# Sample attention: a batch's own tokens weighted through a zeroed 128-wide tile instead of a 16-row slice

## The chip, the cores and the metric

The kernel runs on one core of one Trainium2 chip. The metric is the device time of one execution in microseconds (us). The kernel before took 1886.86 us (median of three runs, 1886.31 to 1892.37).

The names used below: PE is TensorE, DVE is VectorE, ACT is ScalarE, POOL is GpSimd, and SP is the engine that issues nearly all transfers.

## The reference

One step of a two-layer streaming encoder (half-step FFN, a token mixer with four branches, half-step FFN) for 256 prompt frames and for 8 sample streams ("batches") of 16 frames each. The change lies in one branch of the mixer, the latent attention of the sample streams:

```python
def mla_sample(q_nope, q_rope, lat_all, kr_all, w_ukv):
    k_nope, v = mla_expand(lat_all, w_ukv)
    prob = jax.nn.softmax(mla_scores(q_nope, q_rope, k_nope, kr_all), axis=-1).astype(v.dtype)
    return jnp.einsum('bhqk,bkhd->bqhd', prob, v).reshape(b, t, W_A)
# lat_all = concatenate([cache_lat (256 past latents), latent (16 own latents)], axis=1), per batch
```

Each of the 8 batches therefore has 8 heads x 16 frames = 128 query rows, and each row weights 256 cached latents and the 16 latents of its own batch, 256 numbers wide. The products with the key and value matrices are absorbed before and after, so that what is computed per batch is softmax(scores) times latents.

## The kernel before, in words

All 384 frames (256 prompt, 128 sample) go through the layer together. Large products run on PE as three passes of a split in two fp32r halves (`mm3`, line 304): in the trace they are the matmuls `rot<-xh,wh`, `rot<-xh,wl`, `rot<-xl,wh`, 128x384. Every weight block is loaded to a staging buffer by SP (`st`, line 224), cast on ACT (`wh<-st`) and subtracted on DVE (`wl<-st,wh`).

The sample attention is in plain fp32, and one such matmul shows in the trace as two records. The stage lies in `mixer_front`, after the attention of the prompt, and comes once in each layer (from 396 to 460 us and from 1328 to 1392 us). For each batch b (two groups `c` of four):

- `load_ct` (lines 1099 to 1104) loads the cached latents `ct` (256 x 256), and copies the batch's 16 rows of `lat_s` (128 rows: 8 batches x 16) by a transfer into a tile `nl` that begins at partition 0.
- The scores of 128 rows x 272 columns (`acc<-cT,qa`, then `acc<-ck,qrs`) go to one PSUM bank. POOL copies the own latents into the last 16 columns of `cT` before.
- `sample` (line 1109) takes the softmax: row maximum on DVE, exp on ACT, reciprocal and scaling on DVE, into a `half` tile.
- `sample_out` (line 1117) turns the weights: three PE transposes (`acc<-ident,half`, the last one of 16 columns), a copy of 128x256 on ACT and one of 16x128 on DVE to `pTs`; then, for each of two halves of the latent, two matmuls with `ct` over 128 rows and one with `nl` over 16 rows, all three adding up in one PSUM tile; ACT copies the result to `qa`.

The order of work is written out by the program itself: every step is a generator that yields the engine it waits for, and a queue of due times (`tick`, `step`, `ready`, with the costs of `COST` and `LATENCY`) decides at which point of PE's stream it goes on. Between the steps, `fillers` (projections and the first gates, as `rot` passes) run on PE, and the 62 taps of a depthwise convolution (`yTb<-bs,cols,yTb`) fill DVE. The engines PE, ACT, DVE and POOL run in just this order; SP takes its transfers in the order in which they become ready by the planner, and a transfer also waits until the one eight before it has landed, since eight semaphores go round.

Of the kernel before, what the change touches and what calls it, by code (L numbers as in the profile page):

```python
# [8 lines left out]
F32 = mybir.dt.float32  # L9
F32R = mybir.dt.float32r  # L10
BF16 = mybir.dt.bfloat16
AF = mybir.ActivationFunctionType
ALU = mybir.AluOpType
AX = mybir.AxisListType
PSUM = bass.MemoryType.PSUM

P = 128
# [9 lines left out]
S = 16  # L27
NP = TP // S
PAST = 256
# [4 lines left out]
KL = 256  # L34
# [12 lines left out]
PE, ACT, DVE, POOL = "tensor", "scalar", "vector", "gpsimd"  # L47
# [50 lines left out]
class Core:  # L98
# [537 lines left out]
    def mixer_front(self, l, m, mf, ma, aT, yT):  # L636
        nc, tc, a = self.nc, self.tc, self.a
        mm = nc.tensor.matmul
# [10 lines left out]
        lat_s = ma.tile([P, KL], F32, name="lat_s")  # L649
# [187 lines left out]
        with pool("mixq") as mq:  # L837
# [122 lines left out]
            for hp in range(4):  # L960
                w = self.weights(("uq", l, hp))
                for i in range(2):
                    h = 2 * hp + i
                    o = self.bank()[:, :T]
# [22 lines left out]
            for j in range(4):  # L987
                o = self.bank()[:, :TP]
# [5 lines left out]
            for t in range(2):  # L994
                o = self.bank()
# [49 lines left out]
            def load_cT(b, pool=None):  # L1045
                if pool:
                    cTs[b] = pool.tile([P, 2, PAST + S], F32, tag="cT", name="cT", bufs=3)
                else:
                    x = self.gains.tile([P, D], F32, tag="g", name="cT")
                    cTs[b] = x[:, :2 * (PAST + S)].rearrange("p (k s) -> p k s", k=2)  # L1050
                nc.sync.dma_start(out=cTs[b][:, :, 0:PAST], in_=a["cacheT"][l, b])
# [8 lines left out]
            for i in range(4):  # L1060
# [3 lines left out]
                                  in_=krT[64:96, TP:].rearrange("p (c i s) -> p c i s", c=2, i=4)[:, :, i, :])  # L1064
# [9 lines left out]
        with pool("mixs") as ms:  # L1074

            def absorb(k, g, o):
                yield PE
                for i in range(2):
                    dst = qa[:, k].rearrange("p b (h i s) -> p h i b s", h=4, i=2)[:, 2 * g:2 * g + 2, i]
                    src = o[i][:, :2 * P].rearrange("p (h b s) -> p h b s", h=2, b=NB)  # L1080
                    for j in range(2):
                        (nc.vector.tensor_copy if j else nc.scalar.copy)(dst[:, j], src[:, j])

            qa = ms.tile([P, 2, NB, H * S], F32, name="qa")
            for k in range(2):
                for g in range(2):
                    o = [self.bank() for _ in range(2)]
                    for j in range(2):
                        for i in range(2):
                            mm(o[i][:, j * P:(j + 1) * P], lhsT=wkT[i * 64:(i + 1) * 64, 2 * g + j, k * P:(k + 1) * P],  # L1090
                               rhs=qTs[i * 64:(i + 1) * 64, 2 * g + j, :], start=True, stop=True)
                    self.spawn(("qa",), absorb(k, g, o), "acc")
            wuv = ma.tile([P, 2, 512], F32, tag="w", name="wuv")
            nc.sync.dma_start(out=wuv, in_=a["w_ukv"][l, 1])
            self.wait(("qa",), fillers)

            cts = {}

            def load_ct(b):
                ct = ms.tile([P, 2, KL], F32, tag="ct", name="ct", bufs=4)  # L1100
                nc.sync.dma_start(out=ct, in_=a["cache"][l, b].rearrange("(k p) c -> p k c", p=P))
                nl = ms.tile([S, KL], F32, tag="nl", name="nl", bufs=4)
                nc.sync.dma_start(out=nl, in_=lat_s[b * S:(b + 1) * S, :])
                cts[b] = ct, nl

            for b in range(2, 5):
                load_cT(b, ms)

            def sample(b, sb):
                ct, nl = cts.pop(b)  # L1110
                yield PE
                p = self.half()[:, :PAST + S].unsqueeze(1)
                yield from self.softmax(p, sb.unsqueeze(1), 1)
                self.drop("acc")
                self.spawn(("att",), sample_out(b, p, ct, nl))

            def sample_out(b, p, ct, nl):
                yield DVE
                pt = self.acc(2, 0)
                for k in range(2):  # L1120
                    nc.tensor.transpose(pt[:, k * P:(k + 1) * P], p[:, 0, k * P:(k + 1) * P], self.ident)
                nc.tensor.transpose(pt[0:S, 256:384], p[:, 0, PAST:], self.ident)
                self.drop("half")
                yield PE
                ps = ms.tile([P, 3, P], F32, tag="pTs", name="pTs", bufs=2)
                nc.scalar.copy(ps[:, 0:2, :], pt[:, 0:256].rearrange("p (a b) -> p a b", a=2))
                nc.vector.tensor_copy(ps[0:S, 2, :], pt[0:S, 256:384])
                self.drop("acc")
                yield ACT
                o = self.acc(2, 1)[:, :256].rearrange("p (a b) -> p a b", a=2)  # L1130
                for k in range(2):
                    ksl = slice(k * P, (k + 1) * P)
                    for kc in range(2):
                        mm(o[:, k, :], lhsT=ct[:, kc, ksl], rhs=ps[:, kc, :], start=(kc == 0), stop=False)
                    mm(o[:, k, :], lhsT=nl[:, ksl], rhs=ps[0:S, 2, :], start=False, stop=True)
                yield PE
                nc.scalar.copy(qa[:, :, b, :], o)

            for c in range(2):
                sbs = []  # L1140
                for i in range(4):
                    b = 4 * c + i
                    cT = cTs.pop(b)
                    load_ct(b)
                    nc.gpsimd.tensor_copy(cT[:, :, PAST:], latTs[:, :, b * S:(b + 1) * S])
                    sb = self.acc(i // 2, i % 2)[:, :PAST + S]
                    sbs.append(sb)
                    for k in range(2):
                        mm(sb, lhsT=qa[:, k, b, :], rhs=cT[:, k, :], start=(k == 0), stop=False)
                    if 2 <= b < NB - 3:  # L1150
                        load_cT(b + 3, ms)
                    if i == 1:
                        self.pull(fillers, PACE_S)
                for i in range(4):
                    rg = slice(32 * i, 32 * i + 32)
                    mm(sbs[i], lhsT=qrs[rg, c, :], rhs=ck[rg, c, :], start=False, stop=True)
                for i in range(4):
                    self.spawn(("soft",), sample(4 * c + i, sbs[i]), "acc")
                    self.pull(fillers, PACE_S)
                self.wait(("soft",), fillers)  # L1160
            self.wait(("att",), fillers)
            def attended(j, o):
                yield PE
                nc.vector.tensor_copy(aT[:, j, TP:], o)

            for j in range(4):
                o = self.bank()[:, :P]
                for i in range(2):
                    h = 2 * j + i
                    for k in range(2):  # L1170
                        mm(o[i * 64:(i + 1) * 64, :], lhsT=wuv[:, k, h * 64:(h + 1) * 64],
                           rhs=qa[:, k, :, h * S:(h + 1) * S], start=(k == 0), stop=(k == 1))
                self.spawn(("att",), attended(j, o), "acc")
# [311 lines left out]
```

## Time and profile before

| | |
|---|---|
| median of the runs | 1886.86 us |
| the profiled execution | 1885.2 us, its span 1883.4 us |
| PE busy | 1858.1 us (99% of the span) |
| DVE, ACT, POOL busy | 964.1, 693.3, 73.8 us |
| granted PE clock | 0.999 of full speed over the span |

The profile is of one execution. "Busy" of PE counts matmuls that overlap: a record lasts from its start to the end of its pipeline, so that the step from one record to the next, and not the record's length, tells what it costs in a stream. In the timeline, equal records that follow each other are merged into one row with their number.

### The profile page before, as it was taken

To read this page: it belongs to the slowest core of one execution; us is meant where nothing else is said; L and a number is where in the kernel's file an instruction comes from. 1 tells how busy PE (TensorE), PEld (TensorE's weight loads), DVE (VectorE), ACT (ScalarE), POOL (GpSimd) and SP (SyncE) were. 2 spreads that over 40 slices of the span, in tenths; PEclk is the share of its full clock that TensorE was granted. 3 is DMA by queue.
4 is the path that set the end of the run, shared out by engine and by line. 5 is a ranking of instruction groups with operands and counts; after the bars stand their busy time and mean duration, and the time that the engine had idled before them with its cause. 6 is when DMAs were issued, how large, how long until landed. Compare 5 with 4: busy or idle time off the path is not lost.

```text
span 1883.4 us, 25172 instructions
## 1 busy us (share of the span) xinstructions
PE 1858.1 (99%) x10066; PEld 1723.3 (91%) x10066; DVE 964.1 (51%) x1472; ACT 693.3 (37%) x1146; POOL 73.8 (4%) x118
## 2 busy tenths in 40 slices
PE   8999999999999999999999999999999999999998
PEld 6999998978999889999989999988889998999997
DVE  5333347986554463333463333478864445533333
ACT  5333334443333443333343333434343335433332
POOL 0000001300000000000000000013000000000000
PEclk9999999999999999999999999999999999999999
DMA  7434443562334444344443444444514344433441
GB/s 255 132 124 129 128 145 86 149 174 78 107 125 136 145 149 130 126 123 123 134 135 124 133 124 124 126 100 134 174 60 137 121 139 134 146 123 124 128 128 45
DMA packets 99031, 243.12 MB, mean 129 GB/s; under 512 B 29281, under 2 KB 40673, under 8 KB 98914
## 3 DMA queue, kind: packets, MB, share of 16 engines
q1 hardware_dynamic: 98770, 241.45, 41.3%
q8 instruction: 79, 1.29, 0.3%
q14 instruction: 38, 0.31, 0.1%
q10 hardware_dynamic: 144, 0.07, 0.0%
HBM read 237.62 MB, written 3.31 MB: 128 GB/s over the span
## 4 chain that ended last, share of the span: by engine, by line
PE 92%; DVE 6%; ACT 1%; issue 1%; POOL 0%; DMA 0%; POOLq 0%; DVEq 0%; ACTq 0%
PE rot L72 59%; PE acc L72 33%; DVE yTb L72 1%; DVE wl L72 1%; DVE half L72 1%; DVE sx L72 0%; ACT half L72 0%; DVE sv L72 0%; DVE qTp L72 0%; DVE xl L72 0%; DVE yTd L72 0%; DVE qa L72 0%; DVE kT L72 0%; POOL kv L72 0%; ACT qTs L72 0%
## 5 line engine op out<-in xcount | busy, mean ns | idle before, releaser
L72 DVE TENSOR_TENSOR wl<-st,wh 128x1024 fp32r<-128x1024 f32 (+3 forms) x428 | 502.2, 1184 | 481.8 <-ACT wh L72 479.0
L72 ACT CAST wh<-st 128x1024 fp32r<-128x1024 f32 (+3 forms) x428 | 430.6, 1017 | 679.3 <-issue 372.0
L72 PE MATMUL rot<-xh,wh 128*128 128x384 f32 x1984 | 674.7, 340 | 0.8 <-ACT sg L72 0.7
L72 PE MATMUL rot<-xh,wl 128*128 128x384 f32 x1984 | 670.4, 338 | 0.0
L72 PE MATMUL rot<-xl,wh 128*128 128x384 f32 x1984 | 669.9, 338 | 0.0
L72 PEld LDWEIGHTS rot<-xh,wh 128*128 128x128 f32 x1984 | 372.0, 188 | 8.9 <-issue 3.5
L72 PEld LDWEIGHTS rot<-xh,wl 128*128 128x128 f32 x1984 | 372.3, 188 | 4.1 <-issue 0.5
L72 PEld LDWEIGHTS rot<-xl,wh 128*128 128x128 f32 x1984 | 372.1, 188 | 1.1 <-issue 0.5
L72 PE MATMUL acc<-wh,hl 128*128 128x512 f32 x528 | 205.8, 390 | 0.0
L72 PE MATMUL acc<-wl,hh 128*128 128x512 f32 x528 | 205.7, 390 | 0.0
L72 PE MATMUL acc<-wh,hh 128*128 128x512 f32 x528 | 205.5, 389 | 0.0
L72 DVE TENSOR_TENSOR hf<-sg,rot 128x384 f32<-128x384 f32 x80 | 44.4, 555 | 152.5 <-PE rot L72 152.5
L72 PEld LDWEIGHTS acc<-wl,hh 128*128 128x128 f32 x528 | 99.1, 188 | 20.4
L72 PEld LDWEIGHTS acc<-wh,hh 128*128 128x128 f32 x528 | 99.1, 188 | 17.7
L72 PEld LDWEIGHTS acc<-wh,hl 128*128 128x128 f32 x528 | 99.1, 188 | 17.6
L72 ACT ACTIVATE half<-rot 128x384 f32<-128x384 f32 x58 | 28.6, 493 | 167.1 <-PE rot L72 167.1
L72 DVE SCALAR_TENSOR_TENSOR half<-half,acc 128x384 f32<-128x384 f32 x44 | 24.4, 554 | 126.2 <-PE acc L72 126.2
L72 DVE SCALAR_TENSOR_TENSOR yTb<-bs,cols,yTb 128x384 f32<-128x384 f32 x120 | 74.8, 623 | 2.2
L72 POOL TENSOR_TENSOR post<-post,neghalf 128x1 f32<-128x1 f32 x18 | 11.6, 645 | 1455.9 <-DVE post L72 1455.9
L72 PE MATMUL rot<-wl,xh 128*128 128x512 f32 (+1 forms) x144 | 55.8, 388 | 1.5 <-DVE wl L72 1.5
L72 PE MATMUL rot<-wh,xh 128*128 128x512 f32 (+1 forms) x144 | 56.2, 390 | 0.0
L72 PE MATMUL acc<-ident,half 128*128 128x128 f32 (+1 forms) x266 | 43.4, 283 | 7.2 <-DVE half L72 7.2
(211 smaller groups left out, 1665.3 us busy)
## 6 DMA issues: line engine op xcount, KB each, us to landing
st<-ffn_gp SPq DMA_DIRECT2D x160, 512.0 KB, 3.5
st<-ffn_dn SPq DMA_DIRECT2D x88, 512.0 KB, 3.5
st<-in_g SPq DMA_DIRECT2D x64, 512.0 KB, 3.7
st<-in_f SPq DMA_DIRECT2D x24, 512.0 KB, 4.4
st<-ffn_gs SPq DMA_DIRECT2D x16, 512.0 KB, 5.1
st<-w_o SPq DMA_DIRECT2D x16, 512.0 KB, 4.8
st<-w_br SPq DMA_DIRECT2D x16, 384.0 KB, 3.1
st<-in_b SPq DMA_DIRECT2D x8, 512.0 KB, 4.5
```

The lines of the kernel that those rows point to most:

```text
L72: r = f(*args, **kw)
```

## The change

The weights of a batch's own 16 tokens no longer go to the last columns of the `half` tile. They are scaled into columns 16b to 16b+15 of a tile `pn` of 128 x 128, all other columns of which are zero. Its transpose is then 128 rows high, with the 16 rows of the batch at the place that they have in `lat_s`, so the product runs over all 128 rows of `lat_s`, without the copy `nl`. There are four such tiles, cleared once per layer on POOL; batches 4 to 7 use them again and first clear the strip that batch b-4 has left. One ACT copy of 128x384 takes the place of the ACT copy of 128x256 and the DVE copy of 16x128.

```diff
             def load_ct(b):
                 ct = ms.tile([P, 2, KL], F32, tag="ct", name="ct", bufs=4)
                 nc.sync.dma_start(out=ct, in_=a["cache"][l, b].rearrange("(k p) c -> p k c", p=P))
-                nl = ms.tile([S, KL], F32, tag="nl", name="nl", bufs=4)
-                nc.sync.dma_start(out=nl, in_=lat_s[b * S:(b + 1) * S, :])
-                cts[b] = ct, nl
+                cts[b] = ct
...
+            pn = ms.tile([P, 4, P], F32, name="pn")
+            nc.gpsimd.memset(pn, 0.0)
+
             def sample(b, sb):
-                ct, nl = cts.pop(b)
-                yield PE
-                p = self.half()[:, :PAST + S].unsqueeze(1)
-                yield from self.softmax(p, sb.unsqueeze(1), 1)
+                ct = cts.pop(b)
+                yield PE
+                p = self.half()[:, :PAST + S]
+                sx = self.small.tile([P, 3], F32, tag="sx", name="sx")
+                mx, sm, rc = (sx[:, i:i + 1] for i in range(3))
+                own = pn[:, b % 4, :]
+                if b >= 4:
+                    nc.gpsimd.memset(own[:, (b - 4) * S:(b - 3) * S], 0.0)
+                nc.vector.tensor_reduce(mx, sb, axis=AX.X, op=ALU.max, negate=True)
+                yield DVE
+                nc.scalar.activation(p, sb, AF.Exp, bias=mx, accum_out=sm)
+                yield ACT
+                nc.vector.reciprocal(rc, sm)
+                nc.vector.tensor_scalar(p[:, :PAST], p[:, :PAST], rc, None, op0=ALU.mult)
+                nc.vector.tensor_scalar(own[:, b * S:(b + 1) * S], p[:, PAST:], rc, None, op0=ALU.mult)
                 self.drop("acc")
...
-                nc.tensor.transpose(pt[0:S, 256:384], p[:, 0, PAST:], self.ident)
+                for k in range(3):
+                    nc.tensor.transpose(pt[:, k * P:(k + 1) * P], p[:, k * P:(k + 1) * P] if k < 2 else own, self.ident)
...
-                nc.scalar.copy(ps[:, 0:2, :], pt[:, 0:256].rearrange("p (a b) -> p a b", a=2))
-                nc.vector.tensor_copy(ps[0:S, 2, :], pt[0:S, 256:384])
+                nc.scalar.copy(ps, pt.rearrange("p (a b) -> p a b", a=3))
...
-                    for kc in range(2):
-                        mm(o[:, k, :], lhsT=ct[:, kc, ksl], rhs=ps[:, kc, :], start=(kc == 0), stop=False)
-                    mm(o[:, k, :], lhsT=nl[:, ksl], rhs=ps[0:S, 2, :], start=False, stop=True)
+                    for kc in range(3):
+                        mm(o[:, k, :], lhsT=ct[:, kc, ksl] if kc < 2 else lat_s[:, ksl], rhs=ps[:, kc, :],
+                           start=(kc == 0), stop=(kc == 2))
```

PE, layer 0, from the weighted sum of batch 1 to the transposes of batch 2, as a difference (- before, + of the change; `rot` are passes of the fillers, `ident,half` and `ident,pn` transposes, `pTs,...` the weighted sum):

```order
 L72 MATMUL acc<-pTs,ct 128x128 x2
-L72 MATMUL acc<-pTs,nl 128x128
+L72 MATMUL acc<-pTs,lat_s 128x128
 L72 MATMUL acc<-pTs,ct 128x128 x2
-L72 MATMUL acc<-pTs,nl 128x128
-L72 MATMUL rot<-xh,wh 128x384
-L72 MATMUL rot<-xh,wl 128x384
-L72 MATMUL rot<-xl,wh 128x384
+L72 MATMUL acc<-pTs,lat_s 128x128
 L72 MATMUL acc<-ident,half 128x128 x2
-L72 MATMUL acc<-ident,half 16x128
+L72 MATMUL acc<-ident,pn 128x128
```

The number of matmuls and of transposes is the same. Three filler passes that stood between the two batches stand elsewhere in the stream now; all differences on PE lie within the stage.

DVE, layer 0, from the scaling of batch 0 to that of batch 1, as a difference up to the reciprocal of batch 1 (`sx` holds maximum, sum and reciprocal, `yTb` are taps of the convolution):

```order
 L72 RECIPROCAL sx<-sx 128x1
-L72 TENSOR_SCALAR half<-half,sx 128x272
-L72 SCALAR_TENSOR_TENSOR yTb<-bs,cols,yTb 128x384
+L72 TENSOR_SCALAR half<-half,sx 128x256
+L72 TENSOR_SCALAR pn<-half,sx 128x16
 L72 TENSOR_TENSOR yTd<-yTd,rot 128x384
 L72 TENSOR_REDUCE sx<-acc 128x1
-L72 COPY pTs<-acc 16x128
-L72 SCALAR_TENSOR_TENSOR yTb<-bs,cols,yTb 128x384 x2
-L72 RECIPROCAL sx<-sx 128x1
-L72 TENSOR_SCALAR half<-half,sx 128x272
```

In the changed order two taps, one weight split (`wl<-st,wh`) and the two additions `yTc<-rot,gbias` stand after this maximum and ahead of the reciprocal of batch 1; the split stood behind its scaling before. The same happens once more, at batch 5, and both in layer 1 too.

ACT, at the end of the stage, of the change (`half,sx<-acc,sx` is an exp, `pTs` the turned weights of batches 6 and 7, `qa` the results):

```order
L72 COPY pTs<-acc 128x384
L72 CAST wh<-st 128x1024
L72 COPY pTs<-acc 128x384
L72 COPY qa<-acc 128x2x128 x2
```

Before, the same place reads:

```order
L72 CAST wh<-st 128x1024
L72 COPY pTs<-acc 128x256
L72 ACTIVATE half,sx<-acc,sx 128x272
L72 COPY qa<-acc 128x2x128
L72 COPY pTs<-acc 128x256
L72 ACTIVATE sq<-yTb 128x768
L72 COPY qa<-acc 128x2x128
```

The turned weights of batch 7 are copied ahead of the result of batch 6 now, and a cast stands between the two copies of weights. In the same way the cast that stood behind the first result of the stage (batch 0) now stands ahead of the first copy of weights.

On SP the sixteen transfers of `nl` are gone; the load of the gain of the mixer's last norm moves ahead of one load of a gate's weights. On POOL the clearing of `pn` stands ahead of the first copy into `cT`, and the four strips are cleared behind the last one.

## Rows read from the trace of the kernel before

**Rows 1.** The page's first part: busy us, share of the span, instructions.

```profile
span 1883.4 us, 25172 instructions
PE 1858.1 (99%) x10066; PEld 1723.3 (91%) x10066; DVE 964.1 (51%) x1472; ACT 693.3 (37%) x1146; POOL 73.8 (4%) x118
```

**Rows 2.** Windows: us, busy PE, PEld, DVE, ACT, POOL, clock, DMA share, GB/s.

```profile
396.00:460.00 64.00, 61.84 (x404) 50.98 (x404) 48.02 (x114) 19.34 (x49) 2.62 (x4) 1.00 0.48 137
1328.00:1392.00 64.00, 61.84 (x406) 51.05 (x405) 47.76 (x115) 19.11 (x48) 2.65 (x4) 1.00 0.42 127
```

**Rows 3.** Chain of waits, batches 0 to 2: start, us, what.

```profile
417.53 0.33 PE acc L72 x3
417.86 0.88 PE rot L72 x5
418.74 1.91 PE acc L72 x12
420.65 0.72 PE rot L72 x3
421.38 0.33 PE acc L72 x3
```

**Rows 4.** Timeline of PE, batch 1 of layer 0: start, us, what.

```profile
418.58 0.60 PE L72 MATMUL acc<-pTs,ct 128*128 128x128 f32 x4
419.12 0.48 PE L72 MATMUL acc<-pTs,nl 16*128 16x128 f32 x2
419.53 0.71 PE L72 MATMUL acc<-pTs,ct 128*128 128x128 f32 x4
420.17 0.48 PE L72 MATMUL acc<-pTs,nl 16*128 16x128 f32 x2
420.58 0.44 PE L72 MATMUL rot<-xh,wh 128*128 128x384 f32 x1
420.87 0.34 PE L72 MATMUL rot<-xh,wl 128*128 128x384 f32 x1
421.04 0.34 PE L72 MATMUL rot<-xl,wh 128*128 128x384 f32 x1
421.21 0.49 PE L72 MATMUL acc<-ident,half 128*128 128x128 f32 x3
421.46 0.42 PE L72 MATMUL rot<-xh,wh 128*128 128x384 f32 x1
421.72 0.34 PE L72 MATMUL rot<-xh,wl 128*128 128x384 f32 x1
```

**Rows 5.** Tile pTs: durations ns min/median/max.

```profile
L72 PE MATMUL acc<-pTs,ct x128: 270/275/377, 413.6 to 1388.3; 128*128 128x128 f32 x128
L72 PE MATMUL acc<-pTs,nl x64: 270/321/372, 414.2 to 1388.7; 16*128 16x128 f32 x64
```

**Rows 6.** PE's waits in the stage of layer 0: us, times, longest.

```profile
PE acc L72 <- DVE qa L72: 0.9, 1, 0.9
PE acc L72 <- DVE pTs L72: 0.5, 1, 0.5
PE acc L72 <- DVE half L72: 0.4, 1, 0.4
PE rot L72 <- DVE sx L72: 0.4, 1, 0.4
```

**Rows 7.** Groups by form: busy us, mean ns, idle before.

```profile
L72 ACT COPY pTs<-acc 128x256 f32<-128x256 f32 x16 | 6.0, 373 | 13.9 <-PE acc L72 13.7
L72 ACT COPY cg<-rot 128x384 f32<-128x384 f32 x4 | 1.9, 482 | 0.3 <-PE rot L72 0.3
L72 DVE TENSOR_SCALAR half<-half,sx 128x272 f32<-128x272 f32 x16 | 5.8, 361 | 0.6
L72 DVE COPY pTs<-acc 16x128 f32<-16x128 f32 x16 | 4.4, 276 | 14.5 <-ACT pTs L72 14.5
L72 DVE TENSOR_SCALAR half<-half,sx 128x128 f32<-128x128 f32 x16 | 3.5, 282 | 0.4
L72 DVE TENSOR_SCALAR ln<-rot 128x6 f32<-128x6 f32 x1 | 0.2, 165 | 1.2 <-PE rot L72 1.2
L72 POOL MEMSET bd<- 128x512 f32 x2 | 1.1, 535 | 0.0
```

**Rows 8.** Timeline: POOL's first copies into cT, and their first reader.

```profile
391.91 0.51 POOL L72 COPY cT<-latTs 128x32 f32<-128x32 f32 x3 [28.80 <-PE acc L72]
...
400.70 0.62 PE L72 MATMUL acc<-cT,qa 128*128 128x272 f32 x2
```

**Rows 9.** Timeline, batch 4 of layer 0: its scaling and its transposes.

```profile
437.18 0.36 DVE L72 TENSOR_SCALAR half<-half,sx 128x272 f32<-128x272 f32 x1
...
438.06 0.49 PE L72 MATMUL acc<-ident,half 128*128 128x128 f32 x3
```

**Rows 10.** Group: the weight splits on DVE.

```profile
L72 DVE TENSOR_TENSOR wl<-st,wh 128x1024 fp32r<-128x1024 f32 x380 | 463.7, 1223 | 477.1 <-ACT wh L72 475.3 <-issue 0.7
```

**Rows 11.** Tile nl: its transfers, ns of an issue on SP.

```profile
L1103 SPq DMA_DIRECT2D nl<-lat_s x16: 512/576/1110, 400.6 to 1360.7; - x16
```

More of the change, by code (lines that the diff above doesn't have):

```diff
@@ L1101, in load_ct, with sample_out @@
                 nc.sync.dma_start(out=ct, in_=a["cache"][l, b].rearrange("(k p) c -> p k c", p=P))
-                nl = ms.tile([S, KL], F32, tag="nl", name="nl", bufs=4)
-                nc.sync.dma_start(out=nl, in_=lat_s[b * S:(b + 1) * S, :])
-                cts[b] = ct, nl
+                cts[b] = ct
             for b in range(2, 5):
                 load_cT(b, ms)
+            pn = ms.tile([P, 4, P], F32, name="pn")
+            nc.gpsimd.memset(pn, 0.0)
             def sample(b, sb):
-                ct, nl = cts.pop(b)
+                ct = cts.pop(b)
                 yield PE
-                p = self.half()[:, :PAST + S].unsqueeze(1)
-                yield from self.softmax(p, sb.unsqueeze(1), 1)
+                p = self.half()[:, :PAST + S]
[11 more added lines that the diff above has]
+                nc.vector.tensor_scalar(own[:, b * S:(b + 1) * S], p[:, PAST:], rc, None, op0=ALU.mult)
                 self.drop("acc")
-                self.spawn(("att",), sample_out(b, p, ct, nl))
-            def sample_out(b, p, ct, nl):
+                self.spawn(("att",), sample_out(b, p, own, ct))
+            def sample_out(b, p, own, ct):
                 yield DVE
-                pt = self.acc(2, 0)
-                for k in range(2):
-                    nc.tensor.transpose(pt[:, k * P:(k + 1) * P], p[:, 0, k * P:(k + 1) * P], self.ident)
-                nc.tensor.transpose(pt[0:S, 256:384], p[:, 0, PAST:], self.ident)
+                pt = self.acc(2, 0)[:, :3 * P]
+                for k in range(3):
+                    nc.tensor.transpose(pt[:, k * P:(k + 1) * P], p[:, k * P:(k + 1) * P] if k < 2 else own, self.ident)
                 self.drop("half")
```

## The prediction

> **What bounds the kernel now.** I read the page's first part first: PE is busy for 99% of the span, DVE for 51%, ACT for 37% [rows 1]. So a change elsewhere counts only where PE waits, and a change on PE counts in full unless something behind it is late. The windows then show that this also holds in the two stages that the change touches: of 64 us each, PE is busy 61.84, DVE 48.0 and 47.8, and the clock is at the full 2.4 GHz level, 1.00, in both [rows 2]. DVE has 16 us to spare there, a quarter of the stage: enough, but not much. The chain of waits says the same from the other side: through the batches it runs over PE records one after another, transposes (3), fillers (5), the weighted sum of one batch (12 records, 1.91 us), fillers, transposes [rows 3]. The last view is PE's timeline at that weighted sum, where the cost of each kind of record can be read as a step [rows 4].
>
> **The weighted sum on PE.** Per batch it is 12 records before and after: before, eight with `ct` over 128 rows and four with `nl` over 16 rows; after, all twelve over 128 rows. The work looks larger. The steps say otherwise. Four `ct` records last 0.60 us together and one alone about 0.27 [rows 4, 5], so three steps take 0.33 us: 0.11 us a step. Two `nl` records last 0.48 us, so their one step takes 0.21. From one `nl` group to the next thing takes 0.41 us (419.12 to 419.53, 420.17 to 420.58), where two full-height records would take 0.22. And the row behind an `nl` group is longer too: the second group of four `ct` lasts 0.71 instead of 0.60, and the filler behind the last one needs 0.29 us to its successor (420.58 to 420.87) instead of 0.17 (420.87 to 421.04). So each entry into and exit from the 16-row matmuls costs about 0.1 to 0.2 us, twice per batch, whatever they compute.
>
> From the first `ct` record to the second filler pass it is 2.29 us now (418.58 to 420.87) [rows 4]. After the change it should be 12 x 0.11 + 0.17 = 1.49 us, if a full-height fp32 record hands over to a filler without loss. The transposes, which are full-height too, show that: from 421.21 to 421.72 are 0.51 us, and 3 x 0.11 + 0.17 = 0.50 [rows 4]. The difference is 0.80 us; the chain gives the same (1.91 - 1.32 = 0.59 in the sum, 0.72 - 0.51 = 0.21 in the three fillers behind it) [rows 3]. All steps are rounded to 0.01, and a few batches are followed by something other than a filler, so I take 0.78. With 8 batches and 2 layers this is 16 x 0.78 = 12.5 us. If the 0.2 us at the filler stayed, it would be 16 x 0.6 = 9.6; that is the lower bound of this term, 16 x 0.80 = 12.8 the upper.
>
> A rule of the Trainium skill speaks against the change: "TensorEngine Tiling (Array Packing)", Theoretical Speedup, gives a contraction of 32 rows or fewer up to 4 times the speed, so that widening 16 rows to 128 would be a loss. By it a 16-row record would cost a quarter of 0.11 us, and the change would add 64 x 0.08 = 5 us (an estimate from that page). The trace does not agree here: the 16-row step is 0.21 us, twice the full one, since the two records that follow each other use the same rows and have nothing to run beside.
>
> The third transpose turns 128 columns instead of 16. It stays one record of one step in both (0.51 us with a 16-column one in it is what three full steps give) [rows 4]: nothing.
>
> **What DVE, ACT, POOL and SP gain and lose.** DVE drops a copy of 0.276 us per batch and gets a second scaling of 128x16. The trace has no such form; it lies between 128x6 (0.165) and 128x128 (0.282) [rows 7]; I take 0.2, as it is nearest to the small one, and the other scaling gets shorter by a sixteenth column block, nearly nothing. DVE is thus 0.1 us a batch lighter, which shows nowhere by itself. But the pieces lie differently in the chain of a batch:
> - PE waited for the dropped copy once in each layer, 0.5 us [rows 6], and layer 1 has the same row. That goes: -1.0 us. In its place PE waits for the ACT copy alone, which grows from 0.373 to about 0.48 us (a 128x384 copy from PSUM takes 0.482) [rows 7]; fillers stand between in every batch but where said below.
> - The new scaling lies between softmax and transposes. At batch 0, PE already waits 0.4 us for the scaled weights [rows 6], so there it is exposed: 0.2 us in each layer, +0.4 us (bounds 0.33 to 0.56).
> - At batch 4, the scaling ends at 437.54 and the transposes start at 438.06 [rows 9]: 0.52 us of cover. The new order puts the transposes two filler passes (0.34 us) earlier and the scaling 0.2 us later, which leaves nothing: about +0.1 us in each layer, +0.2 us.
> - At the end of the stage the product of batch 7 follows that of batch 6 after four fillers (0.7 us), and both use one PSUM bank, so it waits for ACT to copy the result of batch 6 (0.37 us). That copy now stands behind a cast and the copy of the weights of batch 7, which run while PE computes batch 6 (1.3 us). Between 0 and 0.5 us in each layer; I take 0.2: +0.4 us.
>
> POOL's clearing of `pn` (0.535 us by the same form) [rows 7] waits for a late prompt matmul, just as the copy for batch 2 did at 391.91; the copies for batches 0 and 1, which ran earlier, now queue behind it. Three of them took 0.51 us, so all five end by some 393.4; the first score matmul is at 400.70 [rows 8], 7 us of cover. The strips are small, behind the last copy, and due only when the second half's weights are scaled. Without this cover, each would be 0.5 us at most. SP loses sixteen issues of 0.58 us [rows 11] and as many turns of the eight semaphores, so that later transfers can start sooner. One load of gate weights now stands behind the load of a gain. PE waits for no transfer in the stage [rows 6], so I count neither a gain nor a loss.
>
> **Sum.** -12.5 - 1.0 + 0.4 + 0.2 + 0.4 = -12.5 us against the profiled execution's 1885.2: 1872.7. The median of the runs is 1886.86, 1.7 above, so the forecast for the median is 1886.9 - 12.5 = 1874.4 us. What comes late next: DVE. The taps must be done before the convolution's norm goes to PE, and PE reaches that point, after five batches, some 5 x 0.78 = 4 us earlier in each layer. DVE gets there earlier as well, since it stood waiting for the dropped copies (14.5 us over both layers) [rows 7] while taps were queued behind them; so I see no new wait of more than a few tenths.
>
> **Rivals.**
> 1. *PE becomes free but the softmax chain is the bound.* For it: DVE is busy for 75% of the stage [rows 2], a split of 1.22 us [rows 10] now stands ahead of the reciprocal in two batches of each layer, a cast of like size ahead of a copy of weights in two, and the maxima of all batches queue on the same engine. If the split is exposed in all four places (4.9 us) and the cast in its four for about 1 us each, 9 of the 12.5 us are lost: 1883.4. If half of that is exposed: 1879. Against it: fillers stand between in nearly all batches.
> 2. *The step does not shrink.* If 0.21 us is the price of adding the third product into a bank that has just been written, and not of the 16 rows, the full-height records pay it too. Then only waits change: 1886.9 within 1 us. Against it: the second `ct` pair adds into the same bank at 0.11.
> 3. *Slower: DVE's order makes PE wait at every batch.* Place: between exp and transposes, at the scaling into `pn`, behind whatever split or taps DVE has in hand. Price: one split, 1.22 us, in each of 16 batches: 19.5 us less the 12.5 gives 1886.9 + 7 = 1894. It decides from 0.8 us of new wait per batch on. Against it: in the order the split is there in four batches, not in sixteen.
>
> **How the numbers follow.** Forecast 0.78, rival 1 0.14, rival 2 0.04, rival 3 0.04. Within 0.3% is within 5.7 us, about what a measurement of this kernel can tell from no change. Faster by more: the forecast, and of rival 1 the milder half, 0.78 + 0.06 = 0.84; slower: rival 3, 0.04; same: the rest, 0.12. For the range: all terms at their best give 12.8 + 1.0 and no new wait, 1873, and runs differ by a few tenths to a few us (1886.31 to 1892.37), so I go down to 1869.5; upward to 1883.5, which takes in rival 1 in full.
>
> **What would show it right or wrong.** Right: 12 records `pTs,ct` and `pTs,lat_s` in one row of about 1.5 us with 0.11 us steps, and 0.17 us between the fillers behind; the wait for `pTs` on DVE gone; each stage 6 us shorter with PE still over 95% busy; and nothing changed outside of the stages. Wrong: the same stage length with new rows "PE acc <- DVE pn" or "<- ACT pTs" of several us; or steps of 0.2 us in the `lat_s` records.

## Result and the profile after

The changed kernel takes 1871.7 us (median of four runs, 1871.55 to 1873.1). The kernel before, run beside it, takes 1886.6 us (1885.15 to 1892.37). The ratio is 0.9917 with a 95% interval of 0.9896 to 0.9938, so it is faster. The forecast was 1874.4 us, with a range of 1869.5 to 1883.5. In the profiled executions the span fell by 13.4 us, from 1883.4 to 1870.0; the forecast had 12.5.

The page's first part (busy us, share of the span, instructions) answers to [rows 1]:

```profile
span 1870.0 us, 25153 instructions
PE 1845.8 (99%) x10066; PEld 1719.1 (92%) x10066; DVE 961.3 (51%) x1472; ACT 694.2 (37%) x1146; POOL 76.8 (4%) x128
```

PE has the same number of matmuls and is busy 12.3 us less, still for 99% of the span. So PE was the bound before and is the bound after; its work became cheaper.

The chain of waits (start, us, what) through the batches, as in [rows 3]:

```profile
421.28 1.34 PE acc L72 x12
422.62 0.89 PE rot L72 x5
```

Twelve records of a weighted sum take 1.34 us where they took 1.91, and five fillers behind them 0.89. PE's timeline at one weighted sum (start, us, what) shows why, against [rows 4]:

```profile
421.12 0.60 PE L72 MATMUL acc<-pTs,ct 128*128 128x128 f32 x4
421.56 0.39 PE L72 MATMUL acc<-pTs,lat_s 128*128 128x128 f32 x2
421.78 0.61 PE L72 MATMUL acc<-pTs,ct 128*128 128x128 f32 x4
422.23 0.39 PE L72 MATMUL acc<-pTs,lat_s 128*128 128x128 f32 x2
422.37 0.42 PE L72 MATMUL rot<-xh,wl 128*128 128x384 f32 x1
422.63 0.33 PE L72 MATMUL rot<-xl,wh 128*128 128x384 f32 x1
```

From the first `ct` record to the second filler pass it is 1.51 us (421.12 to 422.63); it was 2.29, and the forecast was 1.49. Read the starts: a pair `lat_s` follows four `ct` after 0.44 and 0.45 us (before: 0.54 and 0.64), and the next thing follows the pair after 0.22 or 0.14 us (before: 0.41). Before, each change of height made two steps about 0.1 us longer, the one onto the first record of the new height and the one behind it: a pair `nl` lasts 0.48 and not 0.39 us, the four `ct` behind it 0.71 and not 0.61.

PE's loads of weights (engine PEld; one load belongs to each matmul) show where these steps lie. Before, then after:

```profile
419.11 0.29 PEld L72 LDWEIGHTS acc<-pTs,nl 16*128 16x128 f32 x2
419.53 0.52 PEld L72 LDWEIGHTS acc<-pTs,ct 128*128 128x128 f32 x4
```

```profile
421.45 0.30 PEld L72 LDWEIGHTS acc<-pTs,lat_s 128*128 128x128 f32 x2
421.67 0.53 PEld L72 LDWEIGHTS acc<-pTs,ct 128*128 128x128 f32 x4
```

After the change, a load begins 0.11 us ahead of its own matmul (421.45 for 421.56, 421.67 for 421.78), while the record before is still running. Before, the first load behind each change of height begins only with its own matmul (419.11 for 419.12, 419.53 for 419.53), so it is not hidden. This holds for the first `nl` load of all 32 pairs. Why the load does not start earlier there, no trace shows.

PE's waits in the stage of layer 0 (us in all, times, longest), against [rows 6]; layer 1 has the same rows:

```profile
PE acc L72 <- DVE qa L72: 0.9, 1, 0.9
PE acc L72 <- DVE pn L72: 0.5, 1, 0.5
PE rot L72 <- DVE sx L72: 0.4, 1, 0.4
```

The wait for `pTs` on DVE is gone. The wait at batch 0 is now for `pn` instead of `half`, and 0.1 us longer. The tiles' groups (ns least/median/most, first and last start) answer to [rows 5, 7]:

```profile
L72 DVE TENSOR_SCALAR pn<-half,sx x16: 226/228/231, 412.4 to 1368.1; 128x16 f32<-128x16 f32 x16
```

```profile
L72 PE MATMUL acc<-pTs,lat_s x64: 275/275/275, 414.9 to 1373.8; 128*128 128x128 f32 x64
L72 ACT COPY pTs<-acc x16: 473/480/490, 413.3 to 1370.7; 128x384 f32<-128x384 f32 x16
```

Where in time it comes from: the n-th pass of the stream of fillers and projections is the same work in both kernels. The one with which both leave the stage of layer 0 starts at 460.44 us before and at 453.84 after, 6.60 us earlier. At the end of the span the passes are 13.4 us earlier, and between the two stages nothing moves by more than 0.2. So each layer's stage gives 6.6 to 6.9 us, and nothing else gives anything clear of these 0.2.

### The profile page after: what moved, and what is told of

Read it like the earlier page. It is cut to its first block, busy times and chain, and to the rows that moved or that the text cites. A ratio compares the mean times of both kernels' runs of the same rounds, so it can differ in the third digit from the quotient of the medians.

```text
span 1870.0 us, 25153 instructions
## 1 busy us (share of the span) xinstructions
PE 1845.8 (99%) x10066; PEld 1719.1 (92%) x10066; DVE 961.3 (51%) x1472; ACT 694.2 (37%) x1146; POOL 76.8 (4%) x128
## 4 chain that ended last, share of the span: by engine, by line
PE 92%; DVE 6%; ACT 1%; issue 1%; POOL 0%; DMA 0%; POOLq 0%; DVEq 0%; ACTq 0%
PE rot L72 59%; PE acc L72 32%; DVE wl L72 1%; DVE yTb L72 1%; DVE half L72 1%; DVE sx L72 0%; DMA st<-ffn_gs 0%; ACT half L72 0%; DVE sv L72 0%; DVE qTp L72 0%; DVE xl L72 0%; DVE yTd L72 0%; DVE qa L72 0%; ACT qTs L72 0%; POOL kv L72 0%
## 5 line engine op out<-in xcount | busy, mean ns | idle before, releaser
L72 PE MATMUL acc<-ident,half 128*128 128x128 f32 x250 | 41.6, 283 | 7.3 <-DVE half L72 6.3
```

The source lines that it names most:

```text
L72: r = f(*args, **kw)
```

## Experiments

The theory under test: PE pays about 0.2 us each time a matmul of fewer rows follows one over 128 rows or the other way round, four times per batch. The rivals: the transfers of `nl`; DVE's copy and the new order; a price of the narrow records themselves.

**The height alone.** The order, transfers and copies of before are kept; `nl` and the third part of `pTs` are 128 rows high, with zeros in the rows that the batch doesn't fill.

```diff
-                    mm(o[:, k, :], lhsT=nl[:, ksl], rhs=ps[0:S, 2, :], start=False, stop=True)
+                    mm(o[:, k, :], lhsT=nl[:, ksl], rhs=ps[:, 2, :], start=False, stop=True)
```

> The kernel before, with only the height of the third product changed: the transfer of the own 16 latents stays, into the first 16 rows of one of four cleared 128-row tiles, and the 16x128 DVE copy stays, into two cleared tiles of turned weights; the product then runs over all 128 rows. Theory (a 16-row product between full-height ones costs PE 0.78 us a batch on entering and leaving it): 16 x 0.78 = 12.5 us faster than before, less at most 1 us, since the waits for the DVE copy stay: span 1871 to 1872, with steps of 0.11 us throughout the weighted sum. Rival A (the gain came from the sixteen transfers that are gone): nothing, 1883. Rival B (it came from the DVE copy and the new order): nothing, 1883.

1874.6 us (1874.28 to 1874.75), ratio 0.9927 [0.9911, 0.9942], span 1872.9. PE's timeline:

```profile
418.08 0.60 PE L72 MATMUL acc<-pTs,ct 128*128 128x128 f32 x4
418.52 0.39 PE L72 MATMUL acc<-pTs,nl 128*128 128x128 f32 x2
418.74 0.61 PE L72 MATMUL acc<-pTs,ct 128*128 128x128 f32 x4
419.19 0.39 PE L72 MATMUL acc<-pTs,nl 128*128 128x128 f32 x2
419.33 0.42 PE L72 MATMUL rot<-xh,wh 128*128 128x384 f32 x1
419.59 0.33 PE L72 MATMUL rot<-xh,wl 128*128 128x384 f32 x1
```

The steps are those of the changed kernel, 1.51 us in all, though the operand is still the transferred `nl`. The height alone gives 10.5 of the 13.4 us of span. That is 0.9 us short of the expected 1871 to 1872. One part of it can be seen: in this order the weighted sum of batch 0 stands between records `rot<-wst,vn` and `rot<-bd,vn` with 64 columns of weights, and its first four `ct` last 0.71 us (from 413.61) in spite of the full height. The rest is open.

**The small copy on ACT.** This is the kernel with the height alone, with `pTs`'s 16x128 copy on ACT behind the large one. It asks what the other 2.9 us are.

```diff
-                nc.vector.tensor_copy(ps[0:S, 2, :], pt[0:S, 256:384])
+                nc.scalar.copy(ps[0:S, 2, :], pt[0:S, 256:384])
```

> The kernel before with full-height products, as in the run of the height alone, and the small copy of turned weights (16x128) on ACT behind the large one instead of on DVE. It tells what the remaining 2.9 us between that run's span (1872.9) and the changed kernel's (1870.0) are. Theory: they are PE's waits for DVE's copy and what these shift: span 1870.0 to 1871, no wait for DVE pTs. Rival: they are the order of the other steps at the ends of the stage: span stays at 1872.5 to 1873, with waits for ACT pTs or DVE half in the place of the one removed.

1872.2 us (1872.07 to 1872.86), ratio 0.9911 [0.989, 0.9932], span 1870.3: as the changed kernel within 0.3 us of span. PE's waits in the stage of layer 0:

```profile
PE acc L72 <- DVE qa L72: 0.9, 1, 0.9
PE acc L72 <- DVE half L72: 0.4, 1, 0.4
```

With the height alone PE also waited for `sx` (0.4) and for `pTs` on DVE (0.3 in layer 0, 0.2 in layer 1). These rows are gone, 1.3 us in both layers; the run is 2.6 us shorter. So the rest of the gain came from taking DVE out of the turning of weights, together with the order that the program then wrote. Half of that 2.6 stands in the waits; which steps of the order hold the other half is open.

**Narrow again, 32 and 64 rows.** The changed kernel, but the third product runs only over the aligned 32 or 64 rows of `lat_s` that hold the batch; the order is the changed kernel's.

```diff
+                    rg = slice(b * S // 32 * 32, b * S // 32 * 32 + 32)
+                    mm(o[:, k, :], lhsT=lat_s[rg, ksl], rhs=ps[rg, 2, :], start=False, stop=True)
```

> The changed kernel, with its third product taken over the 32-row strip of lat_s and of the turned weights that holds the batch's 16 rows; every instruction stands in the same order as in the changed kernel. Theory: the 0.78 us per batch come back, 12.5 us slower than the changed kernel, span 1882 to 1883, about 1 us under the kernel before. Rivals A and B: it stays at the changed kernel's 1870, within 1 us.

> The changed kernel, but the third product runs over the 64 rows of lat_s and of the turned weights in which the batch's own 16 lie, instead of all 128; the order on every engine is that of the changed kernel. Theory: any change of height between neighbouring matmuls costs about 0.2 us, whatever the height is, four times per batch: 16 x 0.78 = 12.5 us lost again, span about 1882.5 against the changed kernel's 1870.0, with one record behind another on the same rows at 0.11 us. Rival: the cost falls with the rows that are left idle (64 instead of 96 or 112 of 128): about half is lost, span about 1876. Second rival: 64 rows count as full height: 1870.

With 32 rows 1883.8 us (1882.95 to 1885.18), ratio 0.9978 [0.9967, 0.9989], span 1882.8; with 64 rows 1883.7 us (1883.21 to 1884.83), ratio 0.9975 [0.9964, 0.9986], span 1881.7. PE's timeline with 32 rows, then with 64:

```profile
419.11 0.60 PE L72 MATMUL acc<-pTs,ct 128*128 128x128 f32 x4
419.65 0.48 PE L72 MATMUL acc<-pTs,lat_s 32*128 32x128 f32 x2
420.06 0.71 PE L72 MATMUL acc<-pTs,ct 128*128 128x128 f32 x4
420.70 0.48 PE L72 MATMUL acc<-pTs,lat_s 32*128 32x128 f32 x2
421.12 0.44 PE L72 MATMUL acc<-ident,half 128*128 128x128 f32 x2
```

```profile
418.99 0.60 PE L72 MATMUL acc<-pTs,ct 128*128 128x128 f32 x4
419.52 0.48 PE L72 MATMUL acc<-pTs,lat_s 64*128 64x128 f32 x2
419.94 0.71 PE L72 MATMUL acc<-pTs,ct 128*128 128x128 f32 x4
420.58 0.48 PE L72 MATMUL acc<-pTs,lat_s 64*128 64x128 f32 x2
```

Both have the durations of the 16-row records in [rows 4] (0.48, 0.71, 0.48), and lose 12.8 and 11.7 us of the 13.4. Counted by the passes of the stream, each stage loses 5.9 to 6.0 us in both runs, 11.8 and 12.0 in all; the run with 32 rows also has a wait of 0.9 us for `half` on DVE between 600 and 700 us, outside of the stages, which the changed kernel's profile doesn't have. The rival by which the price falls with the idle rows (1876) is out: 64 rows cost as much as 32. This undoes the height within the new order and is the mirror of the first run.

**No transfers.** The kernel before without the transfers of `nl`: every batch takes rows 0 to 15 of `lat_s`, which leaves out the own latents of batches 1 to 7.

```diff
-                nl = ms.tile([S, KL], F32, tag="nl", name="nl", bufs=4)
-                nc.sync.dma_start(out=nl, in_=lat_s[b * S:(b + 1) * S, :])
-                cts[b] = ct, nl
+                cts[b] = ct, lat_s[0:S, :]
```

> The kernel before without the sixteen transfers: every batch takes the first 16 rows of lat_s (so batches 1 to 7 use batch 0's own latents, which is left wrong for the sake of the time). Theory: no change within 1 us, 1883. Rival A: most of the 13.4 us that the span lost, 1870 to 1873.

1886.8 us (1884.74 to 1892.07), ratio 0.9997 [0.9984, 1.0011]. The profiled execution has a span of 1886.2 us, and the expectation was 1883 within 1. The granted clock accounts for that: in each of the two stages it stands at its lower level, 1.2 GHz, for 3.4 us (449.3 to 452.7 and 1381.1 to 1384.5), where the profile of before has 1.00. The window in layer 0 (us, busy PE, PEld, DVE, ACT, POOL, clock, DMA share, GB/s):

```profile
449.30:452.65 3.35, 3.35 (x14) 3.11 (x12) 1.78 (x6) 0.85 (x3) 1.13 (x1) 0.50 0.02 5
```

In the 2.4 us before it fell, PE waited 0.39 us for DVE, ran twelve records of two columns each and three fillers; the profile of before has the same rows at 1.00, so what made it fall is open. By the passes behind each stage it costs 1.6 us each time, 3.1 in all, and without it the span is at 1883. So the transfers cost nothing that these runs can tell.

**The narrow products side by side.** The kernel before, but the second half begins with its narrow product, so that the two `nl` pairs follow each other and the height changes twice per batch instead of four times.

```diff
+                    own = lambda: mm(o[:, k, :], lhsT=nl[:, ksl], rhs=ps[0:S, 2, :], start=(k == 1), stop=(k == 0))
+                    if k == 1:
+                        own()
...
+                    if k == 0:
+                        own()
```

> The kernel before, with the two 16-row products of a batch next to each other (first half: two full products, then the narrow one; second half: the narrow one first). Theory in the form that a change of height costs: one entry and one exit per batch instead of two, so half of the 0.78 us goes: 16 x 0.39 = 6.2 us faster, span 1877. Theory in the other form, that each narrow product is slow in itself (0.41 instead of 0.22 us wherever it stands): no gain, 1883.

1879.8 us (1879.65 to 1880.43), ratio 0.9955 [0.9939, 0.9971], span 1877.9, 5.5 less than before: near the 1877 of one form of the theory, far from the 1883 of the other. PE's timeline:

```profile
418.25 0.60 PE L72 MATMUL acc<-pTs,ct 128*128 128x128 f32 x4
418.79 0.71 PE L72 MATMUL acc<-pTs,nl 16*128 16x128 f32 x4
419.43 0.71 PE L72 MATMUL acc<-pTs,ct 128*128 128x128 f32 x4
419.89 0.42 PE L72 MATMUL rot<-xh,wh 128*128 128x384 f32 x1
420.15 0.34 PE L72 MATMUL rot<-xh,wl 128*128 128x384 f32 x1
```

Now 1.90 us from the first `ct` to the second filler (418.25 to 420.15), half of the way from 2.29 to 1.51. And four `nl` records take 0.64 us to the next thing where two took 0.41: the two that came in addition cost 0.115 each. A narrow record therefore costs what a full one does; only the change into the group and out of it is dear.

**Another narrow product.** The changed kernel, and besides it a product outside of the change: in `latent_q` the rotated key is turned by two records with 32 columns of weights between full transposes, six times in all. Here it is one full transpose, of a tile whose last 32 columns POOL clears.

```diff
-                mm(tp[64:96, QL:], lhsT=kro, rhs=self.ident, start=True, stop=True)
+                nc.tensor.transpose(tp[:, QL:], kr.rearrange("p a b -> p (a b)"), self.ident)
```

> The changed kernel, and one other narrow product, in latent_q, is made full height too: the turn of the rotated key (two records over 128x32 columns, written to rows 64 to 95 between transposes, at three places per layer) becomes one transpose of a 128 wide tile whose last 32 columns are cleared on POOL. Theory (a change of the form costs PE about 0.2 us on leaving, whatever it computes): the step out of each of the six places falls from 0.20 to 0.11 us, the step into it likewise, and so about 0.3 to 0.4 us each go: 6 x 0.4 = 2.4 us, span about 1867.5, unless PE waits for POOL's clearing. Rival (only products with fewer rows of contraction pay, and these have 128): nothing, span 1870.0 within 0.5.

> The changed kernel once more, on the same chip as the one with the rope key at full height: 1871.7 us, within a few tenths.

> The changed kernel with the rope key's turn at full height, once more, now beside the changed kernel itself. The trace of its first run shows 0.42 us less at each of the six places (2.5 us in all) with 0.2 to 0.4 us given back elsewhere in each layer, and 1.2 us lost at one place far from them that other runs did not lose. Theory: 1.8 to 2.4 us faster than the changed kernel on this chip. Rival: the difference was one of chips, and both take the same time within 0.5 us.

First run 1869.7 us (1869.38 to 1870.91), ratio to before 0.9898 [0.9882, 0.9915]. Run again, on the same chip as the changed kernel, 1870.1 us (1869.67 to 1871.65), 0.9907 [0.9887, 0.9926], against 1871.7 (1871.62 to 1872.38), 0.9917 [0.99, 0.9933], for the changed kernel. PE's timeline of the changed kernel, then of this one (its first run):

```profile
302.66 0.49 PE L72 MATMUL acc<-ident,half 128*128 128x128 f32 x3
303.08 0.41 PE L72 MATMUL acc<-ident,kr 128*32 128x128 f32 x2
303.42 0.46 PE L72 MATMUL rot<-wh,xl 128*128 128x416 f32 x1
303.71 0.60 PE L72 MATMUL acc<-ident,half 128*128 128x128 f32 x4
```

```profile
302.43 0.49 PE L72 MATMUL acc<-ident,half 128*128 128x128 f32 x3
302.76 0.27 PE L72 MATMUL acc<-ident,kr 128*128 128x128 f32 x1
302.79 0.44 PE L72 MATMUL rot<-wh,xl 128*128 128x416 f32 x1
303.06 0.60 PE L72 MATMUL acc<-ident,half 128*128 128x128 f32 x4
```

From the first transpose to the next ones it is 0.63 us instead of 1.05, 0.42 less, about 0.11 to 0.13 of it the record that is saved. So weights with fewer columns pay a change as well, and the rival (only rows of contraction count) is out for this place. The records of 64 columns in the run with the height alone say the same in another place. Of the whole, 1.6 us side by side and 2.0 in the first run are less than 6 x 0.42 = 2.5. The profile of the first run has a wait of 1.3 us for `half` on DVE between 600 and 700 us. The expectation calls this a loss that other runs did not have; that was wrong, since the run with 32 rows waits 0.9 us there. The runs of the two kernels overlap by one, 1871.65 us, and that is the profiled one: its clock is at 0.50 from 378.5 to 381.7 us. It is the fastest kernel tried; that it beats the changed one by more than runs differ is likely and not settled.

## Why the prediction was right

- **The weighted sum on PE** (-12.5): right, and a little too large. The step is 0.78 us at a batch with fillers behind it, 2.29 to 1.51, and the runs with the height alone (10.5) and with 32 and 64 rows (11.8 and 12.0 in the stages) show it from both sides. These are 0.74 and 0.75 a batch: 0.78 was read at a batch with fillers behind it, and where transposes stand there the changed kernel gains less.
- **The reason given for the narrow step** was wrong. I put the 0.21 us between two `nl` records down to records that use the same rows and have nothing to run beside. With four in a row the additional ones cost 0.115 each; the longer first step is part of the price of the change. The Trainium skill's "TensorEngine Tiling (Array Packing)", Key Properties, says that changing the tiling mode drains TensorE; it gives no price. The traces agree in that each change costs about 0.2 us (0.78 / 4), with 16, 32 or 64 rows; that a mode is what changes here no run shows. The speedup of the same page's table, against which the forecast was weighed, is for small products on different tiles of TensorE at once; it appears nowhere for these products, one after another on the same rows.
- **The wait for `pTs` on DVE** (-1.0): right, both rows are gone.
- **Batch 0** (+0.4): too dear. The scaling into `pn` lasts 0.228 us (I took 0.2), but the other one became shorter and their ends overlap; PE's wait grew from 0.4 to 0.5 us only, +0.2 in both layers by the rounded rows.
- **Batch 4** (+0.2): did not come. DVE's scaling ends at 433.34 (before, in [rows 9]: 437.54), and the transposes start 0.74 us later, where 0.52 us lay between them before (DVE, then PE):

```profile
433.11 0.23 DVE L72 TENSOR_SCALAR pn<-half,sx 128x16 f32<-128x16 f32 x1
```

```profile
434.08 0.38 PE L72 MATMUL acc<-ident,half 128*128 128x128 f32 x2
```

  I moved PE's place by counting its fillers, and added DVE's new work, but left out that DVE comes earlier too: before, it had stood idle for 1.99 and 1.81 us ahead of the copies into `pTs` of batches 2 and 3, and the maximum of batch 4 starts at 431.11 now and not at 434.74. The split of rival 1 stands ahead of the reciprocal of batches 1 and 5, and PE's waits have no row for either. At batch 5 the transposes start at 437.67, 1.1 us behind the scaling, so it is hidden:

```profile
434.76 1.22 DVE L72 TENSOR_TENSOR wl<-st,wh 128x1024 fp32r<-128x1024 f32 x1
435.89 0.16 DVE L72 RECIPROCAL sx<-sx 128x1 f32<-128x1 f32 x1
436.35 0.23 DVE L72 TENSOR_SCALAR pn<-half,sx 128x16 f32<-128x16 f32 x1
```

```profile
437.67 0.38 PE L72 MATMUL acc<-ident,half 128*128 128x128 f32 x2
```

- **Batch 7** (+0.4): did not come. ACT copies the result of batch 6 as soon as it is there, and the product of batch 7 starts behind that (ACT, then PE):

```profile
447.42 0.37 ACT L72 COPY qa<-acc 128x256 f32<-128x256 f32 x1 [0.81 <-PE acc L72]
```

```profile
447.92 0.64 PE L72 MATMUL acc<-pTs,ct 128*128 128x128 f32 x4
```

  ACT had been idle for 0.81 us, so the cast and the copy of weights ahead of it were done: the lower of my two bounds.
- **The sum.** 6.24 for the steps, plus 0.5 for the wait, less 0.1 at batch 0, is 6.6 us a layer, close to the 6.6 to 6.9 of the streams. In part that is luck: with 5.9 to 6.0 for the steps, as the runs with 32 and 64 rows have them, it would be 6.3 to 6.4, and some 0.4 us a layer lie in the new order, for which the forecast had no gain. Of the 0.9 us by which the forecast's 12.5 is short of the span's 13.4, 0.8 are the three stalls priced at 1.0, of which 0.2 came.
- **The other 1.8 us** of the forecast's error lie in the median. I carried over that the median of before is 1.7 above its profiled execution; the changed kernel's is at its own (1871.7 and 1871.77). Runs of before reach up to 1893.5, those of the changed kernel only to 1873.1. Without the transfers they still reach 1892.1, so these are not what scatters. It goes with the granted clock: the runs of before beside the experiments have, at 1890 us and above, a mean of 0.994 to 0.996, all others, up to 1888.1, one of 0.998 or 0.999; the changed kernel's have 0.998 to 1.000. So of the 14.9 us between the medians the work that the change saves accounts for the span's 13.4. Why the clock falls more often before is open. It is not the price of the narrow products itself, which the runs with 32 and 64 rows pay too: all twenty lie between 1882.95 and 1885.18, at 0.998 to 1.000.

The rivals: 1 and 3 are out by the waits, 2 by the steps.

## What to carry to other kernels

Where a small product stands between full ones in a stream that PE bounds, read from the starts what it costs to get into it and out of it, and not only how much it computes: here zeros that filled it up to 128 rows were free. Where it can't be filled up, put the small ones next to each other, which halves the number of changes. When one engine's work is moved earlier, move the engines that waited for it too before pricing a new wait.

## Not expected of the hardware

- Matmuls over 16, 32 and 64 rows cost PE the same change, about 0.2 us in and 0.2 us out, each time as two steps of 0.2 instead of 0.1 us; the load of weights behind the change starts with its matmul and not ahead of it.
- Weights of 32 columns over 128 rows pay as well: 0.42 us at each of six places, one record included.
